# A matmul with RMS norm: the last row block's partial sums written into PSUM before the last product

## The chip, the cores and the metric

One core of one Trainium2 chip. The metric is device time in microseconds (us) of one execution. All runs told of here are of the undisturbed ("fast") state; the granted TensorE clock was 0.989 to 0.994 of full speed in every profiled run.

In the text PE is TensorE, DVE is VectorE, ACT is ScalarE, POOL is GpSimd and SP is SyncE, as the profile names them.

## The reference

```python
# a: 2048 x 2048, b: 2048 x 2048, gamma: 2048, all float32; eps = 1e-5
x = np.matmul(a, b)
rms = np.sqrt(np.mean(x ** 2, axis=-1, keepdims=True) + eps)
return (gamma * x / rms).astype(np.float32)
```

## The kernel before

Rows come in blocks of 128. Most of the product is made by a seven-product scheme: for a pair of row blocks (`ra`, `rb`) and one half of the columns (`j` = 0 left, 1 right), four result chunks x11, x12, x21, x22 of 128 x 512 are put together from seven products of eight matmuls each. `product(g, j, m, bank)` issues product `m` into a PSUM bank; `start=False` lets it accumulate onto what the bank holds. What follows is the end of the last pair, where nothing is left on TensorE to hide behind. `t` (which lives where x22 will be) gathers everything of x22 but products 2 and 6.

```python
# helpers of the last group (DVE unless said otherwise)
def add(out, in0, in1, op=ALU.add):            # one two-tensor operation
    nc.vector.tensor_tensor(out=out, in0=in0, in1=in1, op=op)
def by_r(x, r):                                # ACT: x *= r
    nc.scalar.activation(out=x, in_=x, func=ACTF.Copy, scale=r)
# square(mb, src): ACT squares src and sums along the row into one column of msq[mb]
# scaled_gamma(x, src, r, gam): DVE, x = src * r * gam in one operation
# inverse_rms(last, partial): ACT Sqrt(last + partial), then DVE reciprocal
# partial(mb): DVE adds two columns of msq[mb] and eps

for j in range(2):
    # ... products 5, 1, 4, 3; t[j] = p1 - p5, then + x11 and x12 parts ... [cut]
    p7 = new_bank()
    product(g, j, 7, p7)
    add(x11[j], p7, x11[j])                    # the add that I use as the zero of time
    square(ra, x11[j])
    if j == 0:
        product(g, j, 2, p4[j], start=False)
        nc.scalar.copy(out=x21[j], in_=p4[j])
        square(rb, x21[j])
        add(t[j], t[j], x21[j], ALU.subtract)
        pre_a = partial(ra)
        # ... gamma multiplies ... [cut]
r_a = inverse_rms(msq[ra][:, NCH - 1:NCH], plus(pre_a, ra, 2))
by_r(xa, r_a)
nc.sync.dma_start(out=rows(ra, 0, HALF), in_=xa)
p6 = new_bank()
product(g, 0, 6, p6)
add(x22[0], p6, t[0])
square(rb, x22[0])
nc.gpsimd.tensor_tensor(out=x22[0], in0=x22[0], in1=gam[1], op=ALU.mult)
scaled_gamma(x_tile(ra, 1), x_tile(ra, 1), r_a, gamma_sb[:, HALF:])
nc.sync.dma_start(out=rows(ra, HALF, N), in_=x_tile(ra, 1))
product(g, 1, 2, p4[1], start=False)
add(t[1], t[1], p4[1], ALU.subtract)
square(rb, p4[1])
pre_b = partial(rb)
# ... [cut: `right`, half_sq, two column halves, a new bank p6[h] for each half]
# ... [cut: the last product: per half, eight matmuls 256 wide into p6[h]]
for h, col in enumerate(halves):
    add(x22[1][:, col], p6[h], t[1][:, col])
    nc.gpsimd.tensor_tensor(out=right[:, CH:][:, col], in0=x22[1][:, col],
                            in1=gam[3][:, col], op=ALU.mult)
    # ACT squares x22[1][:, col], row sum into half_sq[:, h]   [cut]
# part = half_sq[:, 0] + pre_b + msq[rb][:, 2]   (DVE)   [cut]
add(right[:, 0:CH], p4[1], gam[2], ALU.mult)
r_b = inverse_rms(half_sq[:, 1:2], part)
by_r(right[:, 0:CH], r_b)
# ... three DVE scalings by r_b, each followed by a store ... [cut]
```

## Time and profile before

| | before |
|---|---|
| median of 6 runs | 222.57 us (222.32 to 222.65) |
| span of the profiled run | 221.2 us |
| PE busy | 210.0 us, 95% |
| last matmul ends | 213.34 us |
| last reciprocal starts | 214.81 us |
| last store issued | 216.32 us |

The head of the profile's page has one row for each engine: busy us, share of the span, number of instructions. The line under the dots is the head of the page's chain of waits (the work that ended last, followed back), as shares of the span by engine.

```profile
PE 210.0 (95%) x1035; PEld 97.7 (44%) x1035; DVE 167.4 (76%) x330; ACT 128.1 (58%) x263; POOL 29.4 (13%) x59
...
PE 83%; DMA 8%; POOL 3%; DVE 2%; issue 1%; ACT 1%; DVEq 0%; ACTq 0%; POOLq 0%
```

TensorE bounds the kernel. The change leaves its matmuls as they are, so only the end can move. The next three fences are the timeline of before in the last 15 us, one for each engine: start (us from the span's start), duration, engine, line of the program, operation, output and input tiles, shape, count, and in brackets the idle time just before and what ended it. `acc` is a PSUM bank. First TensorE:

```profile
206.69 4.91 PE L289 MATMUL acc<-b,s 128*128 128x512 bf16 x22
211.43 1.91 PE L771 MATMUL acc<-b,s 128*128 128x256 bf16 x16
```

ScalarE:

```profile
210.25 1.15 ACT L716 ACTIVATE x<-x,r 128x1024 f32<-128x1024 f32 x1 [0.23 <-DVE r L345]
211.30 0.61 ACT L307 ACTIVATE sq<-x 128x512 bf16<-128x512 f32 x1
211.82 0.19 ACT L307 ACTIVATION_READ_ACCUMULATOR sq<-x 128x1 f32 x1
212.68 0.60 ACT L307 ACTIVATE sq<-acc 128x512 bf16<-128x512 f32 x1 [0.68 <-DVE x L709]
213.18 0.19 ACT L307 ACTIVATION_READ_ACCUMULATOR sq<-acc 128x1 f32 x1
213.40 0.42 ACT L778 ACTIVATE sq<-x 128x256 bf16<-128x256 f32 x1
213.73 0.19 ACT L778 ACTIVATION_READ_ACCUMULATOR sq<-x 128x1 f32 x1
213.94 0.42 ACT L778 ACTIVATE sq<-x 128x256 bf16<-128x256 f32 x1
214.27 0.19 ACT L778 ACTIVATION_READ_ACCUMULATOR sq<-x 128x1 f32 x1
214.49 0.29 ACT L351 ACTIVATE rms<-n,part 128x1 f32<-128x1 f32 x1
```

VectorE:

```profile
208.18 0.69 DVE L709 TENSOR_TENSOR x<-acc,x 128x512 f32<-128x512 f32 x1 [0.42 <-PE acc L289]
...
210.05 0.16 DVE L345 RECIPROCAL r<-rms 128x1 f32<-128x1 f32 x1 [1.11 <-ACT rms L351]
...
213.38 0.42 DVE L709 TENSOR_TENSOR x<-acc,x 128x256 f32<-128x256 f32 x1 [0.26 <-PE acc L771]
213.95 0.27 DVE L781 TENSOR_SCALAR part<-n,part,msq 128x1 f32<-128x1 f32 x1
214.14 0.68 DVE L709 TENSOR_TENSOR a<-acc,gamma_sb 128x512 f32<-128x512 f32 x1
214.81 0.16 DVE L345 RECIPROCAL r<-rms 128x1 f32<-128x1 f32 x1
```

The last add (213.38) starts 0.04 us after the last matmul ends (211.43 + 1.91 = 213.34) and is done at 213.80. But the square that uses it starts at 213.94, just when ScalarE has finished reading out the accumulator of the square before (213.73 + 0.19 = 213.92). So the add is almost hidden already: ScalarE is the limit. And ScalarE is late because it sat idle for 0.68 us before 212.68, waiting for DVE.

### The profile page before, as it was taken

Reading aid. Unit: us, or ns where it says so; the run is one execution under the profiler, and the core shown is the slowest. Engines: PE = TensorE matmul, PEld = TensorE weight load, DVE = VectorE, ACT = ScalarE, POOL = GpSimd, SP = SyncE. Lnnn points to the kernel's source line nnn. Section 1 sums busy time; section 2 is a strip of 40 time slices with the busy share of each in tenths; the row PEclk is TensorE's granted clock in tenths of the full one; section 3 lists DMA queues with packets and bytes.
Section 4 is the critical chain, followed back from the end, with each engine's and each line's share of the span. In section 5 each row is a group of like instructions: output and inputs, shape, how many; then the busy total and the mean of one; then the engine's idle time right before and its main releaser. Section 6 shows DMA issues by size and latency. Waiting matters only on the chain.

```text
span 221.2 us, 3022 instructions
## 1 busy us (share of the span) xinstructions
PE 210.0 (95%) x1035; PEld 97.7 (44%) x1035; DVE 167.4 (76%) x330; ACT 128.1 (58%) x263; POOL 29.4 (13%) x59
## 2 busy tenths in 40 slices
PE   7899899999999999999999999999999999999950
PEld 2445454444455444444444444444444444444430
DVE  2428789999988898969696639855794759797691
ACT  3110001830698898678945997389738995334570
POOL 7634323220000001200110002000200000000040
PEclk9999999999999999999999999999999999999996
DMA  6999999999938596956799249955798349044045
GB/s 184 223 202 209 203 208 210 211 211 238 426 114 357 187 291 120 316 230 150 219 308 397 79 88 266 367 221 95 187 302 367 69 90 381 32 190 193 1 190 191
DMA packets 36321, 47.13 MB, mean 213 GB/s; under 512 B 21969, under 2 KB 26065, under 8 KB 34897
## 3 DMA queue, kind: packets, MB, share of 16 engines
q0 software_dynamic: 9936, 23.33, 41.7%
q1 hardware_dynamic: 25936, 22.29, 33.6%
q10 hardware_dynamic: 432, 1.31, 2.0%
q8 instruction: 8, 0.13, 0.2%
q14 instruction: 9, 0.07, 0.1%
HBM read 34.60 MB, written 16.78 MB: 232 GB/s over the span
## 4 chain that ended last, share of the span: by engine, by line
PE 83%; DMA 8%; POOL 3%; DVE 2%; issue 1%; ACT 1%; DVEq 0%; ACTq 0%; POOLq 0%
PE acc L289 69%; PE acc L384 12%; DMA b<-in_b_dram 8%; POOL early L105 1%; POOL b L99 1%; DVE x L709 1%; PE tbank L415 1%; PE tbank L172 1%; DVE x L712 1%; ACT sq L307 0%; PE tbank L189 0%; PE acc L189 0%; DVE a L709 0%; ACT sq L778 0%; DVE x L786 0%
## 5 line engine op out<-in xcount | busy, mean ns | idle before, releaser
L289 PE MATMUL acc<-b,s 128*128 128x512 bf16 x408 | 92.1, 379 | 0.0
L289 PEld LDWEIGHTS <-s 128*128 128x128 f16 (+1 forms) x512 | 49.9, 98 | 59.9 <-DVE s L264 0.4
L384 PE MATMUL acc<-b,head_at 128*128 128x512 bf16 x176 | 41.9, 379 | 1.0 <-DMA b<-in_b_dram 0.9
L307 ACT ACTIVATE sq<-x 128x512 bf16<-128x512 f32 x54 | 34.0, 630 | 6.9 <-DVE x L709 3.0
L366 DVE SCALAR_TENSOR_TENSOR x<-x,r,gamma_sb 128x1024 f32<-128x1024 f32 x28 | 34.8, 1281 | 0.7
L223 ACT ACTIVATE sq<-a 128x1024 bf16<-128x1024 f32 x24 | 25.3, 1054 | 2.4 <-DMA a<-in_a_dram 1.9
L384 PEld LDWEIGHTS <-head_at 128*128 128x128 bf16 x176 | 16.8, 98 | 20.6 <-issue 1.9
L246 ACT ACTIVATE head_at<-a,s 128x2048 f16<-128x2048 f32 x10 | 20.0, 1998 | 3.7 <-DVE s L233 3.7
L426 ACT COPY x<-acc 128x512 f32<-128x512 f32 x6 | 3.4, 586 | 25.7 <-PE acc L384 25.7
L289 PEld LDWEIGHTS <-head_at 128*128 128x128 f16 (+1 forms) x112 | 10.9, 98 | 13.2
L289 PE MATMUL acc<-early,head_at 128*128 128x512 bf16 x64 | 14.5, 379 | 0.0
L289 PEld LDWEIGHTS <-at_even 128*128 128x128 f16 x96 | 9.4, 98 | 11.3
L289 PE MATMUL acc<-early,s 128*128 128x512 bf16 x56 | 14.4, 379 | 0.0
L264 DVE TENSOR_TENSOR s<-head_at 128x1024 f16<-128x1024 f16 (+5 forms) x22 | 13.4, 635 | 0.1
L596 DVE TENSOR_TENSOR x<-x,x 128x512 f32<-128x512 f32 x9 | 6.2, 692 | 8.8 <-ACT x L594 8.3
L99 POOL DMA_DIRECT2D b<-in_b_dram x15 | 10.6, 706 | 16.0 <-DMA b<-in_b_dram 13.4
L578 ACT COPY x<-acc 128x512 f32<-128x512 f32 x9 | 5.2, 574 | 11.6 <-PE acc L289 11.5
L289 PE MATMUL acc<-t_left,s 128*128 128x512 bf16 x48 | 11.3, 379 | 0.0
L280 DVE TENSOR_TENSOR b<-b 128x1024 bf16<-128x1024 bf16 x16 | 10.8, 684 | 0.2
L289 PE MATMUL acc<-t_left,head_at 128*128 128x512 bf16 x48 | 10.9, 379 | 0.0
L289 PE MATMUL acc<-t_left,at_even 128*128 128x512 bf16 x48 | 10.8, 379 | 0.0
L289 PE MATMUL acc<-early,at_even 128*128 128x512 bf16 x48 | 10.8, 379 | 0.0
(111 smaller groups left out, 216.7 us busy)
## 6 DMA issues: line engine op xcount, KB each, us to landing
out_dram<-x SPq DMA_DIRECT2D x30, 512.0 KB, 3.8
a<-in_a_dram POOLq DMA_DIRECT2D x10, 1024.0 KB, 8.7
b<-in_b_dram POOLq DMA_DIRECT2D x15, 512.0 KB, 17.5
a<-in_a_dram POOLq DMA_DIRECT2D x4, 512.0 KB, 16.6
early<-in_a_dram POOLq DMA_DIRECT2D x7, 256.0 KB, 14.8
early<-in_b_dram ACTq DMA_DIRECT2D x2, 512.0 KB, 5.9
gamma_sb<-in_gamma_dram POOLq DMA_DIRECT2D x1, 1024.0 KB, 14.8
early<-in_a_dram SPq DMA_DIRECT2D x1, 512.0 KB, 5.5
```

Of the source, the lines that this page charges most:

```text
L99: nc.gpsimd.dma_start(out=raw[j][kp], in_=b[kp * W2:(kp + 1) * W2, j * HALF:(j + 1) * HALF].rearrange("(t p) n -> p t n", p=P))
L223: nc.scalar.activation(out=junk, in_=a32[mb][:, h * HALF:(h + 1) * HALF], func=ACTF.Square, scale=2.0 ** -8, accum_out=n2[:, h:h + 1])
L246: nc.scalar.activation(out=a16[mb], in_=a32.pop(mb), func=ACTF.Copy, scale=factor.pop(mb))
L264: nc.vector.tensor_tensor(out=sum_of(g, s)[:, lo:hi, :], in0=x[:, lo:hi, :], in1=y[:, lo:hi, :], op=op)
L280: nc.vector.tensor_tensor(out=flat[:, 1:3, :], in0=flat[:, 1:3, :], in1=flat[:, 0::3, :], op=ALU.add)
L289: nc.tensor.matmul(bank, lhsT[:, kp, :], rhs, start=(start and kp == 0), stop=(kp == KP - 1), skip_group_check=not start)
L307: nc.scalar.activation(out=sq[:, 0:CH], in_=src, func=ACTF.Square, scale=inv_sqrt_n, accum_out=msq[mb][:, c:c + 1])
L366: nc.vector.scalar_tensor_tensor(out=x, in0=x, scalar=inverse_of[mb], in1=gamma_sb[:, h * HALF:(h + 1) * HALF], op0=ALU.mult, op1=ALU.mult)
L384: nc.tensor.matmul(bank, head_at[:, kt, r, :], head_rhs(c, kt), start=(kt == 0), stop=(kt == KT - 1))
L426: copy(out=x_chunk(*g), in_=banks[g])
L578: nc.scalar.copy(out=c, in_=one[1])
L596: nc.vector.tensor_tensor(out=t, in0=t, in1=x12, op=ALU.add)
```

## The change

Its intent is to take the last add off the path behind the last matmul. `t` (with product 2 subtracted) is written by DVE into the PSUM bank beforehand, product 6 accumulates onto it, and the squares and gamma multiplies read the finished result from PSUM. Product 2 of the right half now comes before product 6 of the left half, so that the last product's seeds, which need product 2, are ready in time. GpSimd's three multiplies go to DVE in the change.

The core of the diff (helpers `root` and `inverse_rms` cut; `root` is the Sqrt without the reciprocal):

```diff
-                add(t[j], t[j], x21[j], ALU.subtract)
+                seed = p7
+                add(seed, t[j], x21[j], ALU.subtract)
...
-        r_a = inverse_rms(msq[ra][:, NCH - 1:NCH], plus(pre_a, ra, 2))
+        rms_a = root(msq[ra][:, NCH - 1:NCH], plus(pre_a, ra, 2))
+        product(g, 1, 2, p4[1], start=False)
+        halves = [slice(0, CH // 2), slice(CH // 2, CH)]
+        half = [bank[:, 0:CH // 2] for bank in (p1, p7)]
+        for bank, col in zip(half, halves):
+            add(bank, t[1][:, col], p4[1][:, col], ALU.subtract)
+        r_a = inverse(rms_a)
         by_r(xa, r_a)
         nc.sync.dma_start(out=rows(ra, 0, HALF), in_=xa)
-        p6 = new_bank()
-        product(g, 0, 6, p6)
-        add(x22[0], p6, t[0])
-        square(rb, x22[0])
-        nc.gpsimd.tensor_tensor(out=x22[0], in0=x22[0], in1=gam[1], op=ALU.mult)
+        square(rb, p4[1])
+        product(g, 0, 6, seed, start=False)
         scaled_gamma(x_tile(ra, 1), x_tile(ra, 1), r_a, gamma_sb[:, HALF:])
         nc.sync.dma_start(out=rows(ra, HALF, N), in_=x_tile(ra, 1))
-        product(g, 1, 2, p4[1], start=False)
-        add(t[1], t[1], p4[1], ALU.subtract)
-        square(rb, p4[1])
         pre_b = partial(rb)
+        add(right[:, 0:CH], p4[1], gam[2], ALU.mult)
+        square(rb, seed)
+        add(x22[0], seed, gam[1], ALU.mult)
...
+        for h, (bank, col) in enumerate(zip(half, halves)):
             for kp in range(KP):
                 nc.tensor.matmul(bank, s_sum[6][:, kp, :], b_quarter(1, kp, 0, 1)[:, col],
-                                 start=(kp == 0), stop=(kp == KP - 1))
+                                 start=False, stop=(kp == KP - 1), skip_group_check=True)
-            add(x22[1][:, col], p6[h], t[1][:, col])
-            nc.gpsimd.tensor_tensor(out=right[:, CH:][:, col], in0=x22[1][:, col], ...)
-            nc.scalar.activation(... in_=x22[1][:, col], func=ACTF.Square, ...)
-        add(right[:, 0:CH], p4[1], gam[2], ALU.mult)     # moved: see its + above
+            nc.scalar.activation(... in_=bank, func=ACTF.Square, ...)
+            add(right[:, CH:][:, col], bank, gam[3][:, col], ALU.mult)
+            if h == 0:
+                part = half_sq[:, 0] + pre_b + msq[rb][:, 2]      # shortened; DVE
```

More of the change, by code (lines that the diff above doesn't have):

```diff
@@ L346, in inverse, with root, inverse_rms @@
         return r
-    def inverse_rms(last, partial):
+    def root(last, partial):
         rms = stat_pool.tile([P, 1], FP32, name="rms")
         nc.scalar.activation(out=rms, in_=last, func=ACTF.Sqrt, bias=partial, scale=1.0)
-        return inverse(rms)
+        return rms
+    def inverse_rms(last, partial):
+        return inverse(root(last, partial))
     def rows(mb, lo, hi):
@@ L761, in last_group @@
-        add(t[1], t[1], p4[1], ALU.subtract)
-        square(rb, p4[1])
         pre_b = partial(rb)
         right = a_pool.tile([P, K], FP32, name="a32")[:, 0:HALF]
+        add(right[:, 0:CH], p4[1], gam[2], ALU.mult)
+        square(rb, seed)
+        add(x22[0], seed, gam[1], ALU.mult)
         half_sq = stat_pool.tile([P, 2], FP32, name="n2")
-        halves = [slice(0, CH // 2), slice(CH // 2, CH)]
-        p6 = [new_bank()[:, 0:CH // 2] for _ in halves]
-        for bank, col in zip(p6, halves):
+        part = stat_pool.tile([P, 1], FP32, name="part")
@@ L770, in last_group @@
+        for h, (bank, col) in enumerate(zip(half, halves)):
             for kp in range(KP):
                 nc.tensor.matmul(bank, s_sum[6][:, kp, :], b_quarter(1, kp, 0, 1)[:, col],
-                                 start=(kp == 0), stop=(kp == KP - 1))
-        for h, col in enumerate(halves):
-            add(x22[1][:, col], p6[h], t[1][:, col])
-            nc.gpsimd.tensor_tensor(out=right[:, CH:][:, col], in0=x22[1][:, col],
-                                    in1=gam[3][:, col], op=ALU.mult)
+                                 start=False, stop=(kp == KP - 1), skip_group_check=True)
@@ L777, in last_group @@
             sq = sq_pool.tile([P, 2 * CH], BF16, name="sq")
-            nc.scalar.activation(out=sq[:, 0:CH // 2], in_=x22[1][:, col], func=ACTF.Square,
+            nc.scalar.activation(out=sq[:, 0:CH // 2], in_=bank, func=ACTF.Square,
                                  scale=inv_sqrt_n, accum_out=half_sq[:, h:h + 1])
-        part = stat_pool.tile([P, 1], FP32, name="part")
-        nc.vector.tensor_scalar(out=part, in0=half_sq[:, 0:1], scalar1=pre_b,
-                                scalar2=msq[rb][:, 2:3], op0=ALU.add, op1=ALU.add)
@@ L783, in last_group @@
-        add(right[:, 0:CH], p4[1], gam[2], ALU.mult)
+            add(right[:, CH:][:, col], bank, gam[3][:, col], ALU.mult)
+            if h == 0:
+                nc.vector.tensor_scalar(out=part, in0=half_sq[:, 0:1], scalar1=pre_b,
+                                        scalar2=msq[rb][:, 2:3], op0=ALU.add, op1=ALU.add)
         r_b = inverse_rms(half_sq[:, 1:2], part)
```

## The prediction

> **What bounds the kernel.** TensorE is busy 210.0 of 221.2 us (busy table); the chain that ended last is 83% PE. Nothing of the change touches that part: the number and width of matmuls stay the same, only the order of the last two full products is exchanged. The timeline shows matmuls without a gap until about 213.34 us (last 256-wide one starts 213.07, 272 ns). What can move is the 2.9 us from there to the last store issue (216.32); then 1 MB of stores runs at about 390 GB/s until about 219.1 (windows) and the span ends at 221.2.
>
> **That end today.** After the last matmul: add 0.42 us on DVE (213.38), square 213.94 plus accumulator read to 214.46, Sqrt 214.49, reciprocal 214.81 to 214.97, scalings 215.01 / 215.41 / 215.81, stores 215.53 / 215.97 / 216.32. The last square did not wait for its add (done 213.80) so much as for ScalarE, whose preceding accumulator read ended 213.92. So ScalarE is already the limit there, and dropping the add before it gains about 0.14 us at most.
>
> **What the change removes and adds.** Removed: one 512-wide DVE add (0.67), two 256-wide adds after the last product (0.42 each), one 512-wide subtract (0.68); all POOL multiplies (1.27 and 2 x 0.7, off the chain). Added: two 256-wide seed writes, one 512-wide multiply and two 256-wide multiplies on DVE, all taken from POOL, and one place in order: the reciprocal for row block a now stands behind the seed writes. The Trainium skill, "VectorE: DVE Perf Modes", gives a fp32 two-tensor op (N+151)/0.96 ns: 691 and 424 ns, as the trace has (0.69, 0.42), so I cost the seeds at 0.42, pitch 0.34.
>
> **Schedule by measured pitches** (an estimate from the trace):
> - The second-to-last full product ends about 209.87, as now. Seeds start 209.91 and 210.25; reciprocal of a 210.59 (now 210.05: +0.54).
> - ScalarE: by_r of a 210.79 (now 210.25), square of the product-2 bank 211.84, of the seed bank 212.56 (pitch 0.72), of the halves 213.28 and 213.82 (now 213.40 and 213.94), accumulator read done 214.34. The 0.68 us that ScalarE idled before 212.68 pays for the delay.
> - DVE: scaled gamma 210.79; partial b 212.57 (waits for the square); the multiplies 212.76, 213.36, 213.96; then the `part` sum, placed behind the first half's multiply, 214.30 to 214.57. Sqrt must wait for it: 214.59 instead of 214.49. Reciprocal 214.91 instead of 214.81.
>
> So the expected gain (0.42 us of add plus the hop) goes to ScalarE's queue and to DVE work taken from POOL. Net about +0.1 us; I cannot tell that from zero.
>
> **Prediction: 222.6 us, 8 in 10 between 222.0 and 223.2** (before 222.53). Faster by over 2%: 0.01; within 2%: 0.98; slower: 0.01.
>
> **What would show it.** POOL idle in the last 10 us; no matmul gap longer than today; reciprocal of a about 0.5 us later; no ScalarE gap between by_r and the last square; Sqrt of b released by the `part` sum on DVE rather than by ScalarE; last issue near 216.4; the first two late stores issued closer together (211.97, 212.33), finished before the last megabyte starts.
>
> **What would make it wrong.** DVE writing PSUM could take other than 0.42 us; no such write is in this trace. If ACT and DVE were not kept apart on one bank (today the square of the product-2 bank waits for DVE's read of it), the chain shortens by some tenths. A matmul waiting for a seed (212.30 at the latest for the second half; I expect it ready at 210.7) would lengthen it. Correctness rests on the earlier product in those banks: the Trainium skill, "PSUM — Partial Sum Buffer", rule 2, says accumulation adds onto VectorE's data where an earlier matmul wrote; no run here shows it yet.

## The result and the profile after

| | before | after |
|---|---|---|
| median of 6 runs | 222.57 us (222.32 to 222.65) | 222.62 us (222.29 to 222.85) |
| ratio after / before | | 1.0004, 95% interval 0.9991 to 1.0017 |
| span of the profiled run | 221.2 us | 220.7 us |

Ratios here and below are taken from fast runs. They are neither the ratio of the medians nor quite that of the plain means (for e5 below that would be 1.0007 and not 1.0014). The time did not move. The output is correct.

The head of the page after:

```profile
PE 208.2 (94%) x1015; PEld 97.6 (44%) x1035; DVE 167.3 (76%) x331; ACT 127.9 (58%) x263; POOL 26.7 (12%) x56
...
PE 83%; DMA 8%; POOL 3%; DVE 2%; issue 1%; ACT 1%; DVEq 0%; ACTq 0%; POOLq 0%
```

PE shows 1015 matmuls where there were 1035, but 1035 weight loads as before: 20 records are missing from this trace, no work is. The busy time of PE is therefore not to be compared.

The two profiled executions reach the end at different moments: the add that reads the last product 7, whose code is untouched, starts at 208.18 us before and at 207.54 us after. That 0.64 us arises ahead of it, in code of which the change touches one subtract only (it now writes the left half's seed), and it is no larger than what executions differ by: in the five variants of after that have the same code up to that add (e1 to e4 and e6), it starts anywhere from 207.51 to 208.16 us. So I compare by a yardstick: **from the start of that add to the start of the last reciprocal**. It is 214.81 - 208.18 = 6.63 us before and 214.29 - 207.54 = 6.75 us after. From that reciprocal to the end of the span it is 6.39 us before and 6.41 us after. Each kernel has one profile only; how well such a distance repeats can be seen in a stretch that has the same code in all nine profiles, from that add to the Sqrt of row block a: it takes 1.54 or 1.55 us in each.

The timeline after, TensorE:

```profile
205.83 5.13 PE L289 MATMUL acc<-b,s 128*128 128x512 bf16 x22
210.79 1.91 PE L777 MATMUL acc<-b,s 128*128 128x256 bf16 x16
```

ScalarE:

```profile
210.13 1.15 ACT L719 ACTIVATE x<-x,r 128x1024 f32<-128x1024 f32 x1 [0.75 <-DVE r L345]
211.19 0.57 ACT L307 ACTIVATE sq<-acc 128x512 bf16<-128x512 f32 x1
211.66 0.19 ACT L307 ACTIVATION_READ_ACCUMULATOR sq<-acc 128x1 f32 x1
211.88 0.60 ACT L307 ACTIVATE sq<-acc 128x512 bf16<-128x512 f32 x1
212.38 0.19 ACT L307 ACTIVATION_READ_ACCUMULATOR sq<-acc 128x1 f32 x1
212.60 0.38 ACT L780 ACTIVATE sq<-acc 128x256 bf16<-128x256 f32 x1
212.88 0.19 ACT L780 ACTIVATION_READ_ACCUMULATOR sq<-acc 128x1 f32 x1
213.11 0.38 ACT L780 ACTIVATE sq<-acc 128x256 bf16<-128x256 f32 x1
213.39 0.19 ACT L780 ACTIVATION_READ_ACCUMULATOR sq<-acc 128x1 f32 x1
213.96 0.29 ACT L351 ACTIVATE rms<-n,part 128x1 f32<-128x1 f32 x1 [0.38 <-DVE part L784]
```

VectorE:

```profile
207.54 0.69 DVE L712 TENSOR_TENSOR x<-acc,x 128x512 f32<-128x512 f32 x1 [0.42 <-PE acc L289]
...
209.27 0.76 DVE L712 TENSOR_TENSOR acc<-x,acc 128x256 f32<-128x256 f32 x2 [0.97 <-PE acc L289]
209.94 0.15 DVE L345 RECIPROCAL r<-rms 128x1 f32<-128x1 f32 x1
...
211.89 0.27 DVE L702 TENSOR_SCALAR part<-msq 128x1 f32<-128x1 f32 x1 [0.47 <-ACT sq L307]
212.08 0.68 DVE L712 TENSOR_TENSOR a<-acc,gamma_sb 128x512 f32<-128x512 f32 x1
212.67 0.68 DVE L712 TENSOR_TENSOR x<-acc,gamma_sb 128x512 f32<-128x512 f32 x1
213.27 0.41 DVE L712 TENSOR_TENSOR a<-acc,gamma_sb 128x256 f32<-128x256 f32 x1
213.60 0.27 DVE L784 TENSOR_SCALAR part<-n,part,msq 128x1 f32<-128x1 f32 x1
213.78 0.42 DVE L712 TENSOR_TENSOR a<-acc,gamma_sb 128x256 f32<-128x256 f32 x1
214.29 0.16 DVE L345 RECIPROCAL r<-rms 128x1 f32<-128x1 f32 x1
```

The add behind the last matmul is gone, and so are the 0.68 us for which ScalarE waited on a subtract. Two new waits stand in their place.

- The first: row block a's reciprocal (209.94) is queued on DVE behind the two seed writes, which wait for a product. Its Sqrt had been done since about 209.37. ScalarE idles 0.75 us before the scaling of row block a, where it idled 0.23 us before, and all its squares follow from there. The last square starts 213.11, which is 0.41 us behind the last matmul's end (210.79 + 1.91 = 212.70). It needs nothing but that matmul: it waits for ScalarE's own queue.
- The second: the Sqrt waits 0.38 us for `part`, a 0.27 us sum that DVE takes up behind three multiplies, of which two were GpSimd's (212.67 and 213.27) and one was DVE's own and stood behind `part` before (212.08).

### The profile page after: what moved, and what is told of

Same layout as the page of the kernel before. It is cut to its first block, busy times and chain, and to the rows that moved or that the text cites. A ratio compares the mean times of both kernels' runs of the same rounds, so it can differ in the third digit from the quotient of the medians.

```text
span 220.7 us, 2998 instructions
## 1 busy us (share of the span) xinstructions
PE 208.2 (94%) x1015; PEld 97.6 (44%) x1035; DVE 167.3 (76%) x331; ACT 127.9 (58%) x263; POOL 26.7 (12%) x56
## 4 chain that ended last, share of the span: by engine, by line
PE 83%; DMA 8%; POOL 3%; DVE 2%; issue 1%; ACT 1%; DVEq 0%; ACTq 0%; POOLq 0%
PE acc L289 69%; PE acc L387 12%; DMA b<-in_b_dram 8%; POOL early L105 1%; POOL b L99 1%; PE tbank L418 1%; PE tbank L172 1%; DVE a L712 0%; PE tbank L189 0%; PE acc L189 0%; ACT x L719 0%; DVE acc L712 0%; ACT sq L307 0%; DVE x L712 0%; DVE x L788 0%
## 5 line engine op out<-in xcount | busy, mean ns | idle before, releaser
L387 PE MATMUL acc<-b,head_at 128*128 128x512 bf16 x171 | 41.2, 379 | 0.6 <-DMA b<-in_b_dram 0.2
L307 ACT ACTIVATE sq<-x 128x512 bf16<-128x512 f32 x53 | 33.4, 630 | 6.9 <-DVE x L712 3.0
```

The lines of the kernel that those rows point to most:

```text
L307: nc.scalar.activation(out=sq[:, 0:CH], in_=src, func=ACTF.Square, scale=inv_sqrt_n, accum_out=msq[mb][:, c:c + 1])
L387: nc.tensor.matmul(bank, head_at[:, kt, r, :], head_rhs(c, kt), start=(kt == 0), stop=(kt == KT - 1))
```

## The experiments

My theory: the end is paced by ScalarE's queue and by the order of work on DVE. The add that the change removes was hidden by ScalarE, and what the change opens up is given back by the two waits just named. There are three rivals. *Rival 1*: the stores at the end set the time, and the arithmetic ahead of them does not matter. *Rival 2*: the multiplies taken over from GpSimd are the whole loss, whatever their order. *Rival 3*: the removed add had been on the chain, as the change supposed, and the hand-over of the seeds to TensorE costs it back.

Seven kernels ran in two batches, each on one chip with runs of the kernel before. The kernel after was in neither batch, so it is compared with them through its own ratio to before. The `Kernel` column uses the names under which the expectations are quoted.

| Kernel | add to reciprocal, us | reciprocal to end, us | median, us | ratio to before (95%) |
|---|---|---|---|---|
| before | 6.63 | 6.39 | 222.57 | 1 |
| after | 6.75 | 6.41 | 222.62 | 1.0004 (0.9991 to 1.0017) |
| e1_part_early | 6.58 | 6.36 | 222.59 | 0.9992 (0.9980 to 1.0004) |
| e2_recip_first | 6.23 | 6.34 | 222.15 | 0.9972 (0.9960 to 0.9984) |
| e3_all_three | 6.09 | 6.29 | 222.19 | 0.9974 (0.9962 to 0.9986) |
| e4_defer | 6.41 | 6.37 | 222.32 | 0.9984 (0.9972 to 0.9996) |
| e5_no_swap | 6.79 | 6.43 | 222.68 | 1.0014 (1.0000 to 1.0028) |
| b1_no_last_adds (wrong result) | 6.56 | 6.43 | 222.56 | 0.9999 (0.9987 to 1.0012) |
| e6_both_orders | 6.11 | 6.38 | 221.77 | 0.9969 (0.9957 to 0.9982) |

In the first batch (e1 to e4) the kernel before had a median of 222.74 us, in the second 222.51. Spans are printed to 0.1 us, so the third column is good to 0.05 us. All outputs were correct except that of b1.

### b1_no_last_adds: the kernel before, last adds left out

```diff
         for h, col in enumerate(halves):
-            add(x22[1][:, col], p6[h], t[1][:, col])
...
-            nc.scalar.activation(out=sq[:, 0:CH // 2], in_=x22[1][:, col], func=ACTF.Square,
+            nc.scalar.activation(out=sq[:, 0:CH // 2], in_=p6[h], func=ACTF.Square,
```

> The kernel before with the two 256-wide adds after the last product simply left out (wrong result on purpose: ScalarE squares the bare product in PSUM, GpSimd multiplies the old t). My theory: the removed 0.42 us add was covered by ScalarE's queue, so removing it gains under 0.1 us: yardstick 6.55 us (before 6.63), time as before. Rival (the add and its hop were on the chain, as the change supposed): yardstick 6.15 to 6.2, time 0.2% under before.

Measured: 6.56 us, 0.07 under before; ratio 0.9999. This is the most direct statement about the change's intent: removing the last adds outright, at no cost, gains 0.07 us and no time that the runs can show. The ScalarE timeline of this kernel says why:

```profile
212.41 0.60 ACT L307 ACTIVATE sq<-acc 128x512 bf16<-128x512 f32 x1 [0.68 <-DVE x L709]
212.91 0.19 ACT L307 ACTIVATION_READ_ACCUMULATOR sq<-acc 128x1 f32 x1
213.13 0.38 ACT L777 ACTIVATE sq<-acc 128x256 bf16<-128x256 f32 x1
213.41 0.19 ACT L777 ACTIVATION_READ_ACCUMULATOR sq<-acc 128x1 f32 x1
213.64 0.38 ACT L777 ACTIVATE sq<-acc 128x256 bf16<-128x256 f32 x1
```

The last matmul ends here at 211.16 + 1.91 = 213.07 (its start and duration from this kernel's timeline), yet the last square starts at 213.64. ScalarE is busy without a gap from 212.41. Even the 0.07 us is not the add's: the two last squares now read PSUM, take 0.38 us where they took 0.42, and so ScalarE's queue moves on 0.51 us for each where it moved 0.54 and 0.55. The first half of rival 3 falls.

### e1_part_early: `part` ahead of the multiplies

```diff
-            add(right[:, CH:][:, col], bank, gam[3][:, col], ALU.mult)
             if h == 0:
                 nc.vector.tensor_scalar(out=part, in0=half_sq[:, 0:1], scalar1=pre_b,
                                         scalar2=msq[rb][:, 2:3], op0=ALU.add, op1=ALU.add)
+            add(right[:, CH:][:, col], bank, gam[3][:, col], ALU.mult)
```

> The kernel after, with only the `part` sum moved ahead of the first half's gamma multiply. Yardstick: start of the last reciprocal minus start of the DVE add that reads the last block's product-7 bank (before 214.81 - 208.18 = 6.63 us; after 214.29 - 207.54 = 6.75 us). My theory (the end is paced by DVE's order of work and by ScalarE's queue): the Sqrt no longer waits for `part`, it starts when ScalarE's last accumulator read is done, 0.36 us earlier; but the reciprocal then stands behind the second half's multiply, so it moves only about 0.16 us: yardstick 6.59 us, time about 0.1% under the kernel after. Rival 1 (the stores at the end set the time, whatever the arithmetic does): the yardstick may fall, the stretch from the reciprocal to the end (6.41 us after, 6.39 before) grows by as much and the time does not move. Rival 2 (the multiplies taken over from GpSimd are the whole loss, their order is not): yardstick stays 6.75.

Measured: 6.58 us. The wait of the Sqrt for `part` is gone from the list of waits, and the Sqrt follows ScalarE's own last read-out, 6.09 us behind the add at 208.16 where after has 6.42:

```profile
214.25 0.29 ACT L351 ACTIVATE rms<-n,part 128x1 f32<-128x1 f32 x1
214.74 0.15 DVE L345 RECIPROCAL r<-rms 128x1 f32<-128x1 f32 x1
```

As expected the reciprocal gains less than the Sqrt, because it stands behind the second half's multiply: it starts 0.20 us after the Sqrt's end (214.54), in after 0.04. The ratio of 0.9992 lies on the expected side of after's 1.0004, but the intervals overlap, so by time alone it shows nothing.

### e2_recip_first: row block a's reciprocal ahead of the seeds

```diff
+        r_a = inverse(rms_a)
         for bank, col in zip(half, halves):
             add(bank, t[1][:, col], p4[1][:, col], ALU.subtract)
-        r_a = inverse(rms_a)
```

> The kernel after, with only the reciprocal of row block a moved ahead of the two seed writes. My theory: ScalarE's scaling of row block a starts 0.54 us earlier, all its squares follow, the last square then waits for TensorE (starts about 0.04 us after the last matmul ends) and not for ScalarE; DVE's multiplies move up too, the Sqrt still waits for `part`. Yardstick 6.18 us (after 6.75, before 6.63), stretch from reciprocal to end unchanged at 6.4, time about 0.25% under the kernel after and 0.2% under the kernel before. Rival 1 (stores set the end): yardstick falls, time stays. Rival 2 (only the number of DVE multiplies counts): yardstick about 6.75, time as after. A matmul that waits for the later seeds would show as a gap before the first 256-wide matmul; I expect none (seeds ready 0.5 us ahead).

Measured: 6.23 us (expected 6.18), and 0.28% under before with the whole interval below 1, and below after's. No gap on TensorE: the first 256-wide matmul starts 3.26 us behind the add (3.25 in before and after). One line moved, nothing removed: rival 2 expected 6.75 and falls. The stretch behind the reciprocal stayed (6.34 us) and the time went down with the yardstick, so rival 1 falls too, as far as the reciprocal is concerned. The end of ScalarE's work in this kernel:

```profile
212.90 0.38 ACT L780 ACTIVATE sq<-acc 128x256 bf16<-128x256 f32 x1 [0.24 <-PE acc L777]
213.18 0.19 ACT L780 ACTIVATION_READ_ACCUMULATOR sq<-acc 128x1 f32 x1
213.53 0.29 ACT L351 ACTIVATE rms<-n,part 128x1 f32<-128x1 f32 x1 [0.16 <-DVE part L784]
```

Now the last square waits for TensorE, as the change meant it to. The wait for `part` remains, 0.16 us.

### e6_both_orders: both lines moved

The edits of e1 and e2 together, nothing else.

> The kernel after with the two reorderings alone: reciprocal of row block a ahead of the seeds, `part` ahead of the gamma multiplies; no fused operation. Nothing of DVE's work is removed. My theory: yardstick 6.09 us as the kernel with the fused operation, stretch from reciprocal to end 6.35, time 0.25% to 0.3% under before. If the number of multiplies mattered and not their order, it would stay at 6.23 or above.

Measured: 6.11 us, ratio 0.9969. This version beats both kernels, by 0.31% of before (median 221.77 us against 222.51 in its batch), with DVE doing just what it does after, in another order. ScalarE and DVE at its end:

```profile
212.77 0.38 ACT L780 ACTIVATE sq<-acc 128x256 bf16<-128x256 f32 x1 [0.25 <-PE acc L777]
213.05 0.20 ACT L780 ACTIVATION_READ_ACCUMULATOR sq<-acc 128x1 f32 x1
213.28 0.29 ACT L351 ACTIVATE rms<-n,part 128x1 f32<-128x1 f32 x1
```

```profile
213.62 0.15 DVE L345 RECIPROCAL r<-rms 128x1 f32<-128x1 f32 x1
```

The last matmul ends at 212.68 (210.77 + 1.91), the last square starts 0.09 us later; before, it was 0.60 us later (213.94 - 213.34). That difference of 0.51 us accounts for the yardstick's fall from 6.63 to 6.11.

### e3_all_three: both, and one multiply fused behind the reciprocal

```diff
-            add(right[:, CH:][:, col], bank, gam[3][:, col], ALU.mult)
             if h == 0:
                 ... part ...
+                add(right[:, CH:][:, col], bank, gam[3][:, col], ALU.mult)
...
-        nc.vector.tensor_scalar_mul(out=right[:, CH:], in0=right[:, CH:], scalar1=r_b)
+        h0, h1 = (right[:, CH:][:, col] for col in halves)
+        nc.vector.tensor_scalar_mul(out=h0, in0=h0, scalar1=r_b)
+        scaled_gamma(h1, half[1], r_b, gam[3][:, halves[1]])
```
(with the edit of e2)

> The kernel after with the reciprocal of row block a ahead of the seeds, `part` ahead of the multiplies, and the second half's gamma multiply fused with its scaling behind the last reciprocal. My theory: everything left between the last matmul and the last reciprocal is square 0.38, accumulator read, Sqrt 0.29 and the hops: yardstick 6.01 us, 0.62 under before, 0.74 under after; the stretch from reciprocal to end grows by 0.1 to 0.2 us because the fused operation is in it; time 0.2% to 0.3% under before. Rival 1: time as before within noise. Rival 2: yardstick drops by no more than the one multiply moved away (0.34).

Measured: 6.09 us, 0.08 above the expected 6.01; ratio 0.9974. Most of the miss is a hand-over that I had set too short: the last square starts 0.10 us after the last matmul's end, where I had taken the 0.04 us that DVE needs for the same in before. The fused multiply gains nothing over e6 (6.11) that could be told apart. The stretch behind the reciprocal did not grow as expected (6.29).

### e4_defer: GpSimd's former multiplies off DVE until behind the reciprocal

```diff
-        add(x22[0], seed, gam[1], ALU.mult)
...
-            add(right[:, CH:][:, col], bank, gam[3][:, col], ALU.mult)
...
-        nc.vector.tensor_scalar_mul(out=right[:, CH:], in0=right[:, CH:], scalar1=r_b)
+        for bank, col in zip(half, halves):
+            scaled_gamma(right[:, CH:][:, col], bank, r_b, gam[3][:, col])
...
-        nc.vector.tensor_scalar_mul(out=xb[:, CH:], in0=xb[:, CH:], scalar1=r_b)
+        scaled_gamma(xb[:, CH:], seed, r_b, gam[1])
```

> The kernel after with all three gamma multiplies that GpSimd did before (one 512 wide, two 256 wide) taken off DVE until behind the last reciprocal, where they are fused with the scaling; the reciprocal of row block a stays behind the seeds. My theory: DVE has `part` ready at once, the Sqrt starts when ScalarE's delayed queue is done: yardstick 6.38 us, so this is worth 0.37 of the 0.74 that the third kernel of this batch gains, and the rest is ScalarE's delay. The stretch behind the reciprocal grows by 0.2 to 0.5 us, so the time is about as after. Rival 2 (the multiplies are the whole loss): yardstick 6.0, as the third kernel. Rival 1: time not over after by more than noise even though the last DVE operation ends about 0.5 us later behind the reciprocal.

Measured: 6.41 us. With all three multiplies away, the yardstick falls by 0.34 and not to the 6.1 of e3 and e6: the rest is ScalarE's delay, which the reciprocal's place causes. Its last square still starts 0.41 us behind the last matmul's end (211.18 + 1.91 = 213.09), as in after:

```profile
213.50 0.38 ACT L779 ACTIVATE sq<-acc 128x256 bf16<-128x256 f32 x1
```

Rival 2 falls a second time.

One expectation here was wrong. The last DVE operation now ends 2.13 us behind the reciprocal (215.72 + 0.74 - 214.33) against 1.47 us after (215.28 + 0.48 - 214.29), and the last store is issued 2.16 us behind it against 1.51. Yet the stretch to the end is 6.37 us, as everywhere, where I had expected it to grow by 0.2 to 0.5 us. (The time is 0.16% under before; its interval overlaps that of after, so a difference between these two is not shown.) So rival 1 holds in a part: behind the reciprocal, the last scalings have at least some 0.6 us of slack. In all nine profiles the first of the three last stores is issued 0.71 us behind the reciprocal (0.70 to 0.72), and the end follows 6.3 to 6.4 us behind the reciprocal. That the bytes queued behind that first store set the end is argued from this, and from the 390 GB/s at which the last 1 MB runs; no run here moved the first store alone, so it stays open.

### e5_no_swap: the products in their old order, seeds late

The edit: `product(g, 0, 6, seed, start=False)`, `square(rb, seed)` and the store of row block a first, then `product(g, 1, 2, p4[1], start=False)`, the two seed writes, `square(rb, p4[1])` and the multiply of `seed`; row block a's reciprocal ahead of all this.

> The kernel after with the order of the last two full products undone (product 6 of the left half first, as before) and the reciprocal of row block a ahead of the seeds, which now come late. Same yardstick (after 6.75, before 6.63, reciprocal-first with the swap 6.23 us). My theory: here the seeds do hold TensorE: the product that they subtract ends only with the last full product, so the first 256-wide matmul starts about 0.7 us late (3.98 us behind the DVE add that reads product 7, in place of 3.25) and the gap passes through to the end: yardstick 6.79 us, time about as after or 0.1% over it. Rival (a seed hand-over costs TensorE nothing, since an accumulating product only needs its bank): no gap, yardstick near 6.2.

Measured: 6.79 us; ratio 1.0014 (1.0000 to 1.0028). TensorE in this kernel:

```profile
211.32 1.91 PE L777 MATMUL acc<-b,s 128*128 128x256 bf16 x16 [0.52 <-DVE acc L712]
```

It idles 0.52 us for a seed, and the first 256-wide matmul starts 3.94 us behind the add of the yardstick in place of 3.25. This is what the swap of the two products is for. It also settles the second half of rival 3: a seed can cost TensorE time, and in the kernel after it does not, since there the first 256-wide matmul shows no idle time.

## Why the prediction was right

It predicted 222.6 us and within 2%, and 222.62 us came. That the two agree to 0.02 us is luck, since the six runs spread over 0.56 us, and a forecast of no change is met by many mechanisms. What matters more is whether the steps hold. Times from the start of the yardstick's add, in us; the predicted ones are the prediction's times less 208.18, the measured ones those of the profile after less 207.54:

| step | predicted | measured |
|---|---|---|
| first seed write | 1.73 | 1.73 |
| reciprocal of row block a | 2.41 | 2.40 |
| square of the product-2 bank | 3.66 | 3.65 |
| square of the seed bank | 4.38 | 4.34 |
| last square | 5.64 | 5.57 |
| `part` | 6.12 | 6.06 |
| Sqrt | 6.41 | 6.42 |
| last reciprocal | 6.73 | 6.75 |
| second store of row block a | 4.15 | 4.61 |

That the last reciprocal fits to 0.02 us is in part luck: `part` came 0.06 us earlier than forecast, and the Sqrt followed 0.36 us behind its start where 0.29 was forecast.

- **What bounds the kernel** was right: the chain of waits is 83% PE before and after.
- **"dropping the add before it gains about 0.14 us at most"** held as a bound, and was tested by itself: 0.07 us in b1. As reasoning it is loose: 0.14 us is the time for which the finished add lay waiting for ScalarE, not a gain to be had from dropping it. What b1 gained came from shorter squares.
- **The reciprocal of row block a "+0.54"**: measured +0.53 (2.40 against 210.05 - 208.18 = 1.87). e2 shows what it costs: 0.52 us of yardstick.
- **Sqrt released by `part` on DVE**: right, 0.38 us; e1 shows that it costs 0.17 us of yardstick.
- **"Net about +0.1 us"**: +0.12 us on the yardstick. The runs can't tell this from zero (1.0004, 0.9991 to 1.0017), as the prediction said.
- **VectorE writing PSUM** was an unknown in it. The two seed writes took 0.76 us together, which is one of 0.42 and a pitch of 0.34, as into SBUF. The formula of the Trainium skill, "VectorE: DVE Perf Modes", in the section on the TRN2 errata, (N+151)/0.96 ns, gives an estimate of 424 ns for 256 columns; the two writes are recorded with 422 and 428 ns each, so it held for PSUM as the output too.
- **Accumulating onto VectorE's data** was the other. The Trainium skill, "PSUM — Partial Sum Buffer", rule 2, says that a matmul without the start flag adds to such data where an earlier matmul wrote, and overwrites it where an earlier start flag left the place unwritten. All three seeded banks had held a full product. The outputs of after and of all six variants of it that ran (e1 to e6) are correct, which agrees; no run tested a bank without an earlier product.
- **ACT and DVE kept apart on one bank**: they are. In e5 the second half's multiply on DVE is released by ScalarE's square of the same bank (it starts at 213.83, after 0.19 us of idle time that the square ended). The same page, section "PSUM bank collisions raise a hardware error", says why a program must do so even for two readers; no run here lets them collide.
- **Wrong**: the second store of row block a was predicted "issued closer together". It was issued 0.84 us behind the first, as in before (0.85), although its data was ready at 211.41 and it went out at 212.15. Its data had moved before that of the last stores began to (between 215.0 and 215.5 us the DMA engines moved only 25 GB/s, in the stretches about it some 390), so it cost nothing that these runs show.

The prediction named a cost in each of the two orders but treated them as part of the change. The experiments show that they are separable: the change in a good order is worth 0.52 us on the yardstick (e6 against before), and the order in which it was put gave back 0.64 us (after against e6). How much of the 0.52 us is the seeding itself is argued and not shown: e6 also has the two products swapped and the multiplies on DVE, and no run reordered the kernel before alone. From before's profile I estimate that order alone could bring at most 0.14 us there, since the last add is done at 213.80 and its square starts at 213.94; the rest would need the add to be gone.

## What to carry to other kernels

Before taking an operation off the end of a chain, look at whether its consumer started when it ended or when its own engine came free; here the two were 0.14 us apart, and removing the operation outright gained 0.07 us. In these traces each engine took its work in the order of the program, ready or not (row block a's reciprocal waited 0.57 us on DVE with its Sqrt done), so a small operation that another engine waits for (a reciprocal of 0.16 us, a sum of 0.27 us) must not be queued behind work that waits for something else or that nobody needs yet. When a seed for an accumulation depends on another product, let a third product run between the two, or TensorE waits for the seed (0.52 us in e5, nothing in e2).

## What the Trainium skill lacked or had wrong

- "ScalarE: Activation LUTs" gives 186 ns + 0.833 ns per column for an ACTIVATE with immediate operands (section "What ACT_TABLE_LOAD costs"), an estimate of 612 ns for 512 columns, and the trace agrees (0.61 to 0.63 us from SBUF, 0.57 to 0.60 from PSUM). It mentions the accumulator output, but not that it is an instruction of its own: the read-out is 0.19 us long, and squares with row sums follow one another at 0.72 us for 512 columns (212.68 to 213.40), where 612 - 93 = 519 ns is an estimate from that page without it.
- The same page's formula gives an estimate of 399 ns for 256 columns, whatever memory is read. Squares of 256 columns took 0.42 us from SBUF and 0.38 us from PSUM (before and after). This is a gap of that page only; elsewhere the skill counts the two sources apart.
- No page that I read gives the hand-over from TensorE by consumer: DVE started 0.04 us after the last matmul's end in before, ScalarE 0.09 to 0.10 us after it in e2, e3, e5 and e6. The ends of matmuls are modelled in the profile, so only the difference counts.
- No page that I read gives the pitch at which SyncE issues stores: the record of the first 512 KB store of row block a is 0.33 us long, but the second one started 0.84 us after the first in after, with its data ready 0.74 us earlier. The two are 0.84 or 0.85 us apart in all nine profiles. In after the view of waits names DVE's sum `pre_b` (211.89 + 0.27; the profile calls it part) as what released the second; in e5 the store was issued ahead of that sum and at the same pitch, so the sum is not the cause. It is no fixed pitch of SyncE either: behind the first of the last stores (256 KB) the next came 0.44 us later. The cause stays open.
